# Gather, cumulative sum and projection: groups of 512 rows, a gather that converts to fp16 in flight, and stores in runs of 8 KB

## The chip, the cores and the metric

The kernel runs on one core of a Trainium2 chip. The metric is the device time of one execution in microseconds (us), as the median of several runs. Engines are named as in the profile: PE multiplies matrices, DVE and ACT are the vector and the scalar engine, POOL issues the gathers, SP issues plain transfers, and 16 DMA engines move the data.

## The reference

```
x: (16, 4096, 512) fp32    indices: (16, 2048) int64, sorted in each batch    w: (512, 512) fp32
gathered = x[b_idx, indices, :]          # (16, 2048, 512)
cs = np.cumsum(gathered, axis=1)         # along the 2048 rows
return np.matmul(cs, w)                  # (16, 2048, 512) fp32
```

67.1 MB of rows of 2 KB are gathered, and 67.1 MB of output are written.

## The kernel before

A batch of 2048 rows is 16 tiles of 128 rows. For each of the 16 batches the program makes three passes over its tiles.

- POOL gathers a tile's 128 rows of 2 KB into one slot of `g32` (L79), and ACT copies the slot to fp16, `g16` (L86). `g32` holds a whole batch and has two buffers, so the first gather of a batch waits until all casts of the batch two before it are done.
- PE multiplies each of four column blocks of `g16` with the upper triangular `ut` (L93, four matmuls of 128 columns). That gives the tile's cumulative sum, transposed, in the PSUM tile `pa`. DVE adds the last column of the tile before and writes fp16 `csT` (L106; L103 for the first tile, a plain copy). So the tiles of a batch form a chain on DVE.
- PE multiplies the four column blocks of `csT` with `w16` (L116, four matmuls of 512 columns, summed in `pb`). `pb` is copied to `ob` by DVE for even tiles (L125) and by ACT for odd ones (L127). SP stores `ob`, 128 rows of 2 KB (L128). There are 12 `ob` buffers.

The indices of a batch come as 16 rows of 128, are converted to fp32 (L62), transposed on PE (L64) and copied to unsigned integers (L66). Four batches are loaded before the loop and one more in each turn, on SP's queue behind the load of `w` (L51, cast on DVE at L52).

The framework puts each engine's instructions in order by priority, and each engine runs its own in that order. The adds have a raised priority (L101), so that they and the cumulative sums of a batch stand among the projections of the same batch; the last 22 projection matmuls of a batch stand behind all of its cumulative sums.

Of the kernel before, what the change touches and what calls it, by code (L numbers as in the profile page):

```python
# [1 line left out]

# [5 lines left out]

P = 128  # L10
FP32 = mybir.dt.float32
FP16 = mybir.dt.float16
U32 = mybir.dt.uint32


@with_exitstack
def kernel(
    ctx: ExitStack,
    tc: tile.TileContext,
    x: bass.AP,  # L20
    indices: bass.AP,
    w: bass.AP,
    out: bass.AP,
):
    nc = tc.nc

    B, S, D = x.shape
    N = indices.shape[1]
    assert D == 512 and N % P == 0

    NT = N // P
    DC = D // P
    PREF = 3

    x_flat = x.rearrange("b s d -> (b s) d")
    idx_u32 = indices.bitcast(U32)

    const = ctx.enter_context(tc.tile_pool(name="const", bufs=1))
    idxp = ctx.enter_context(tc.tile_pool(name="idxp", bufs=6))
    gp = ctx.enter_context(tc.tile_pool(name="gp", bufs=2))  # L40
    big = ctx.enter_context(tc.tile_pool(name="big", bufs=2))
    outp = ctx.enter_context(tc.tile_pool(name="outp", bufs=12))
    psA = ctx.enter_context(tc.tile_pool(name="psA", bufs=2, space=bass.MemoryType.PSUM))
    psB = ctx.enter_context(tc.tile_pool(name="psB", bufs=5, space=bass.MemoryType.PSUM))

    ut = const.tile([P, P], FP16)
    make_upper_triangular(nc, ut[:], 1.0, diag=True)

    w16 = const.tile([P, DC, D], FP16)
    w32 = const.tile([P, DC, D], FP32)  # L50
    nc.sync.dma_start(out=w32[:], in_=w.rearrange("(c p) d -> p c d", p=P))  # L51
    nc.vector.tensor_copy(out=w16[:], in_=w32[:])  # L52

    id16 = const.tile([16, 16], FP32)
    make_identity(nc, id16[:])
    idxgs = {}

    def load_indices(b):
        idx64 = idxp.tile([16, P], mybir.dt.int64, name="idx64")
        nc.sync.dma_start(out=idx64[:], in_=indices[b].rearrange("(t p) -> t p", p=P))  # L60
        idxf = idxp.tile([16, P], FP32, name="idxf")
        nc.vector.tensor_copy(out=idxf[:], in_=idx64[:].bitcast(U32)[:, 0::2])  # L62
        idx_ps = psB.tile([P, 16], FP32, name="idx_ps", tag="pb")
        nc.tensor.transpose(out=idx_ps[:], in_=idxf[:], identity=id16[:])  # L64
        idxg = idxp.tile([P, NT], U32, name="idxg")
        nc.vector.tensor_copy(out=idxg[:], in_=idx_ps[:])  # L66
        idxgs[b] = idxg

    for bb in range(4):
        load_indices(bb)  # L70

    for b in range(B):
        if b + 4 < B:
            load_indices(b + 4)
        idxg = idxgs.pop(b)
        g32 = gp.tile([P, NT, D], FP32, name="g32")
        g16 = big.tile([P, NT, D], FP16, name="g16")
        for t in range(NT):
            nc.gpsimd.indirect_dma_start(  # L79
                out=g32[:, t, :],  # L80
                out_offset=None,
                in_=x_flat,
                in_offset=bass.IndirectOffsetOnAxis(ap=idxg[:, t : t + 1], axis=0),
                element_offset=b * S * D,
            )
            nc.scalar.copy(out=g16[:, t, :], in_=g32[:, t, :])  # L86

        csT = big.tile([P, DC, N], FP16, name="csT")

        for t in range(NT):  # L90
            pa = psA.tile([P, DC * P], FP32, name="pa")
            for c in range(DC):
                nc.tensor.matmul(  # L93
                    out=pa[:, c * P : (c + 1) * P],
                    lhsT=g16[:, t, c * P : (c + 1) * P],
                    rhs=ut[:],
                    start=(c == 0),
                    stop=(c == DC - 1),
                )
            pa3 = pa[:].rearrange("p (c n) -> p c n", c=DC)  # L100
            with tc.high_priority(offset=200):  # L101
                if t == 0:
                    nc.vector.tensor_copy(out=csT[:, :, 0:P], in_=pa3)  # L103
                else:
                    carry = csT[:, :, t * P - 1 : t * P].broadcast_to([P, DC, P])
                    nc.vector.tensor_tensor(  # L106
                        out=csT[:, :, t * P : (t + 1) * P],
                        in0=pa3,
                        in1=carry,
                        op=mybir.AluOpType.add,  # L110
                    )

        for t in range(NT):
            pb = psB.tile([P, D], FP32, name="pb")
            for c in range(DC):
                nc.tensor.matmul(  # L116
                    out=pb[:],
                    lhsT=csT[:, c, t * P : (t + 1) * P],
                    rhs=w16[:, c, :],
                    start=(c == 0),  # L120
                    stop=(c == DC - 1),
                )
            ob = outp.tile([P, D], FP32, name="ob")
            if t % 2 == 0:
                nc.vector.tensor_copy(out=ob[:], in_=pb[:])  # L125
            else:
                nc.scalar.copy(out=ob[:], in_=pb[:])  # L127
            nc.sync.dma_start(out=out[b, t * P : (t + 1) * P, :], in_=ob[:])  # L128


# [1 line left out]
_INS = ['x', 'indices', 'w']  # L132
_OUTS = [((16, 2048, 512), 'float32')]


# [23 lines left out]
```

## Time and profile before

| | us |
|---|---|
| median of 3 runs (lowest, highest) | 381.35 (379.84, 381.68) |
| the profiled execution, its span | 595.4 |
| POOL busy issuing gathers | 242.8 |
| PE busy | 359.3 |
| DVE busy | 260.1 |
| ACT busy | 208.7 |
| mean granted clock of PE, as a share of full | 0.776 |

The profiled execution's own time is its span, 595.4 us; it is 1.56 times the median of the runs. Busy times are those of the profiled execution. Durations in the rows below are from it as well.

### The profile page before, as it was taken

To read this page: it belongs to the slowest core of one execution; us is meant where nothing else is said; L and a number is where in the kernel's file an instruction comes from. 1 tells how busy PE (TensorE), PEld (TensorE's weight loads), DVE (VectorE), ACT (ScalarE), POOL (GpSimd) and SP (SyncE) were. 2 spreads that over 40 slices of the span, in tenths; PEclk is the share of its full clock that TensorE was granted. 3 is DMA by queue.
4 is the path that set the end of the run, shared out by engine and by line. 5 is a ranking of instruction groups with operands and counts; after the bars stand their busy time and mean duration, and the time that the engine had idled before them with its cause. 6 is when DMAs were issued, how large, how long until landed. Compare 5 with 4: busy or idle time off the path is not lost.

```text
span 595.4 us, 6309 instructions
## 1 busy us (share of the span) xinstructions
PE 359.3 (60%) x2064; PEld 177.9 (30%) x2064; DVE 260.1 (44%) x417; ACT 208.7 (35%) x385; POOL 243.7 (41%) x264
## 2 busy tenths in 40 slices
PE   0413653746464791829558284582855838559997
PEld 0201231323232341414224142241422414225553
DVE  2202352425253572516327163361642717339885
ACT  1302353333160453307034070350703507045722
POOL 3772737372717254450714507236072360710000
PEclk9855967566969895868759677596785968869999
DMA  4774969584859678674857748568385684855565
GB/s 141 215 223 143 296 220 295 165 314 162 284 192 307 222 268 293 225 220 177 290 179 243 243 164 288 183 231 263 149 295 187 216 279 189 290 197 211 214 233 227
DMA packets 58416, 135.96 MB, mean 228 GB/s; under 512 B 8464, under 2 KB 8720, under 8 KB 58384
## 3 DMA queue, kind: packets, MB, share of 16 engines
q0 software_dynamic: 20480, 67.13, 37.2%
q1 hardware_dynamic: 37904, 68.44, 30.7%
q8 instruction: 16, 0.26, 0.2%
q14 instruction: 16, 0.13, 0.1%
HBM read 68.42 MB, written 67.11 MB: 228 GB/s over the span
## 4 chain that ended last, share of the span: by engine, by line
PE 49%; another core or an unknown queue 32%; issue 8%; DVE 7%; DMA 2%; POOL 1%; ACT 1%; DVEq 0%; ACTq 0%
PE pb L116 38%; PE pa L93 11%; DVE csT L106 3%; DVE csT L103 2%; DVE ob L125 2%; DMA w<-in_w_dram 1%; POOL g L79 1%; DMA g<-in_x_dram,idxg 1%; ACT ob L127 0%; ACT g L86 0%; DVE w L52 0%; PE idx_ps L64 0%; DVE idxf L62 0%; DVE idxg L66 0%
## 5 line engine op out<-in xcount | busy, mean ns | idle before, releaser
L79 POOL DMA_INDIRECT g<-in_x_dram,idxg x256 | 242.8, 949 | 280.0 <-ACT g L86 198.7
L116 PE MATMUL pb<-w,csT 128*128 128x512 f16 x1024 | 307.6, 434 | 18.9 <-DVE ob L125 13.1
L106 DVE TENSOR_TENSOR csT<-pa,csT 128x512 f16<-128x512 f32 x240 | 165.3, 689 | 148.9 <-remote 91.0
L93 PE MATMUL pa<-ut,g 128*128 128x128 f16 x1024 | 109.0, 238 | 196.1 <-DVE csT L106 91.9
L127 ACT COPY ob<-pb 128x512 f32<-128x512 f32 x128 | 75.1, 586 | 352.6 <-remote 163.8
L93 PEld LDWEIGHTS <-g 128*128 128x128 f16 x1024 | 81.7, 106 | 278.5 <-issue 188.1
L125 DVE COPY ob<-pb 128x512 f32<-128x512 f32 x128 | 87.7, 688 | 164.1 <-remote 87.9
L86 ACT CAST g<-g 128x512 f16<-128x512 f32 x256 | 141.8, 620 | 29.9 <-DMA g<-in_x_dram,idxg 16.5
L116 PEld LDWEIGHTS <-csT 128*128 128x128 f16 x1024 | 103.3, 110 | 111.6 <-issue 61.3
L64 PE MATMUL idx_ps<-id,idxf 16*128 16x16 f32 x16 | 3.4, 252 | 17.1 <-DVE idxf L62 8.3
L103 DVE CAST csT<-pa 128x512 f16<-128x512 f32 x16 | 11.0, 690 | 6.0 <-remote 2.6
L64 PEld LDWEIGHTS idx_ps<-id,idxf 16*128 16x128 f32 x16 | 2.3, 158 | 22.8 <-issue 11.4
L62 DVE CAST idxf<-idx 16x128 f32<-16x128 uint32 x16 | 3.2, 215 | 2.6 <-DMA idx<-in_indices_dram 2.4
L52 DVE CAST w<-w 128x2048 f16<-128x2048 f32 x1 | 1.2, 1227 | 6.8 <-DMA w<-in_w_dram 6.8
L66 DVE CAST idxg<-idx_ps 128x16 uint32<-128x16 f32 x16 | 2.5, 171 | 2.8 <-PE idx_ps L64 2.4
L86 ACT ACT_TABLE_LOAD x1 | 1.3, 1283 | 0.7 <-PEq L143 0.7
masks.py:65 POOL MEMSET ut<- 128x128 f16 x1 | 0.2, 205 | 0.3 <-POOLq L143 0.3
masks.py:66 POOL TENSOR_SCALAR_AFFINE_SELECT ut<-ut 128x128 f16<-128x128 f16 x1 | 0.3, 284 | 0.0
L143 POOL MEMSET const-float32-0.0<- 128x1 f32 x1 | 0.1, 104 | 0.2 <-issue 0.2
masks.py:199 POOL TENSOR_SCALAR_AFFINE_SELECT id<-id 16x16 f32<-16x16 f32 x1 | 0.2, 190 | 0.0
L143 POOL MEMSET const-uint8-127<- 128x1 uint8 x1 | 0.1, 124 | 0.0
L143 POOL MEMSET const-bfloat16-1.0<- 128x1 bf16 x1 | 0.1, 118 | 0.0
(2 smaller groups left out, 0.2 us busy)
## 6 DMA issues: line engine op xcount, KB each, us to landing
out_dram<-ob SPq DMA_DIRECT2D x256, 256.0 KB
g<-in_x_dram,idxg POOLq DMA_INDIRECT x256
w<-in_w_dram SPq DMA_DIRECT2D x1, 1024.0 KB
idx<-in_indices_dram SPq DMA_DIRECT2D x16, 16.0 KB
```

Of the source, the lines that this page charges most:

```text
L52: nc.vector.tensor_copy(out=w16[:], in_=w32[:])
L62: nc.vector.tensor_copy(out=idxf[:], in_=idx64[:].bitcast(U32)[:, 0::2])
L64: nc.tensor.transpose(out=idx_ps[:], in_=idxf[:], identity=id16[:])
L66: nc.vector.tensor_copy(out=idxg[:], in_=idx_ps[:])
L79: nc.gpsimd.indirect_dma_start(out=g32[:, t, :], out_offset=None, in_=x_flat, in_offset=bass.IndirectOffsetOnAxis(ap=idxg[:, t : t + 1], a ...
L86: nc.scalar.copy(out=g16[:, t, :], in_=g32[:, t, :])
L93: nc.tensor.matmul(out=pa[:, c * P : (c + 1) * P], lhsT=g16[:, t, c * P : (c + 1) * P], rhs=ut[:], start=(c == 0), stop=(c == DC - 1),)
L103: nc.vector.tensor_copy(out=csT[:, :, 0:P], in_=pa3)
L106: nc.vector.tensor_tensor(out=csT[:, :, t * P : (t + 1) * P], in0=pa3, in1=carry, op=mybir.AluOpType.add,)
L116: nc.tensor.matmul(out=pb[:], lhsT=csT[:, c, t * P : (t + 1) * P], rhs=w16[:, c, :], start=(c == 0), stop=(c == DC - 1),)
L125: nc.vector.tensor_copy(out=ob[:], in_=pb[:])
L127: nc.scalar.copy(out=ob[:], in_=pb[:])
```

## The change

These things are different, and the diff below holds them.

- The tiles of all batches form one sequence of 256, in 64 groups of four (512 rows). There are no passes by batch any more.
- The gather writes fp16 `g16` tiles directly from fp32 `x`; `g32` and ACT's casts are gone. There are 48 buffers of one tile. Ten groups (40 gathers) are issued before the loop, and one more group in each turn.
- The triangular `ut` has its columns permuted: column (r, q) sums the rows up to 4q + r of the tile. `csT` of a group is laid out so that the projection with index r uses the rows 4p + r of the group's 512 rows, for p from 0 to 127. Each partition of the output then holds four neighbouring rows.
- In the loop, the cumulative sum of tile r of group g stands ahead of projection r of group g - 1, in program order.
- `pa` has three buffers in place of two. DVE does all adds and no output copies.
- ACT does all output copies, into one `ob` tile of four rows per partition.
- A store takes the whole group, 1 MB with runs of 8 KB, from SP. There are five `ob` buffers.
- The indices come in two loads of 128 x 128, are converted, transposed and copied before the loop.
- `w` is loaded on ACT's queue and cast on ACT.

```diff
-    idxp = ctx.enter_context(tc.tile_pool(name="idxp", bufs=6))
-    gp = ctx.enter_context(tc.tile_pool(name="gp", bufs=2))
-    big = ctx.enter_context(tc.tile_pool(name="big", bufs=2))
-    outp = ctx.enter_context(tc.tile_pool(name="outp", bufs=12))
-    psA = ctx.enter_context(tc.tile_pool(name="psA", bufs=2, space=bass.MemoryType.PSUM))
+    gp = ctx.enter_context(tc.tile_pool(name="gp", bufs=R * (AHEAD + 2)))      # R = 4, AHEAD = 10
+    csp = ctx.enter_context(tc.tile_pool(name="csp", bufs=4))
+    outp = ctx.enter_context(tc.tile_pool(name="outp", bufs=5))
+    psA = ctx.enter_context(tc.tile_pool(name="psA", bufs=3, space=bass.MemoryType.PSUM))
...
+    for k in range(KI):                                                        # KI = 2
+        nc.sync.dma_start(out=idx64[:, k, :], in_=idx_rows[k * P : (k + 1) * P, :])
+    nc.scalar.dma_start(out=w32[:], in_=w.rearrange("(c p) d -> p c d", p=P))
+    make_identity(nc, ident[:])
+    nc.gpsimd.memset(ut[:], 1.0)                                               # ut: [P, R, Q], Q = 32
+    nc.gpsimd.affine_select(out=ut[:], in_=ut[:], compare_op=mybir.AluOpType.is_ge, fill=0.0,
+        base=0, pattern=[[1, R], [R, Q]], channel_multiplier=-1)
+    for k in range(KI):
+        nc.vector.tensor_copy(out=idxf[:, k, :], in_=idx64[:, k, :].bitcast(U32)[:, 0::2])
+        idx_ps = psB.tile([P, P], FP32, name="idx_ps", tag="pb")
+        nc.tensor.transpose(out=idx_ps[:], in_=idxf[:, k, :], identity=ident[:])
+        nc.vector.tensor_copy(out=idxg[:, k, :], in_=idx_ps[:])
-    nc.vector.tensor_copy(out=w16[:], in_=w32[:])
+    nc.scalar.copy(out=w16[:], in_=w32[:])
...
+    def gather(g):
+        for r in range(R):
+            t = g * R + r
+            g16 = gp.tile([P, D], FP16, name="g16")
             nc.gpsimd.indirect_dma_start(
-                out=g32[:, t, :],
+                out=g16[:],
...
-            nc.scalar.copy(out=g16[:, t, :], in_=g32[:, t, :])
...
+    def cumsum_tile(g, r):
+        pa = psA.tile([P, DC, R, Q], FP32, name="pa")
+        for c in range(DC):
+            nc.tensor.matmul(out=pa[:, c], lhsT=g16[:, c * P : (c + 1) * P], rhs=ut[:],
+                start=(c == 0), stop=(c == DC - 1))
+        dst = csT[:, :, :, r * Q : (r + 1) * Q]
...
+        nc.vector.tensor_tensor(out=dst, in0=pa[:],
+            in1=last.unsqueeze(2).broadcast_to([P, DC, R, Q]), op=mybir.AluOpType.add)
...
+    def project_tile(g, r):
+        for c in range(DC):
+            nc.tensor.matmul(out=pb[:], lhsT=csT[:, c, r, :], rhs=w16[:, c, :],
+                start=(c == 0), stop=(c == DC - 1))
+        nc.scalar.copy(out=obs[g][:, r, :], in_=pb[:])
+        if r == R - 1:
+            b, h = divmod(g, GB)                                               # GB = 4 groups in a batch
+            dst = out[b, h * R * P : (h + 1) * R * P, :].rearrange("(p j) d -> p j d", j=R)
+            nc.sync.dma_start(out=dst, in_=obs.pop(g)[:])
...
+    for g in range(AHEAD):
+        gather(g)
+    for g in range(G + 1):                                                     # G = 64
+        if g + AHEAD < G:
+            gather(g + AHEAD)
+        for r in range(R):
+            if g < G:
+                cumsum_tile(g, r)
+            if g > 0:
+                project_tile(g - 1, r)
```

## Rows read from the trace of the kernel before

**Rows 1.** The page: its first line, span and number of instructions.
```profile
span 595.4 us, 6309 instructions
```

**Rows 2.** Timeline of POOL, last 16 gathers: start us, us, instruction, idle time before.
```profile
504.58 0.94 POOL L79 DMA_INDIRECT g<-in_x_dram,idxg  x1 [15.26 <-ACT g L86]
505.83 0.94 POOL L79 DMA_INDIRECT g<-in_x_dram,idxg  x1 [0.30 <-issue]
...
523.38 0.95 POOL L79 DMA_INDIRECT g<-in_x_dram,idxg  x1 [0.30 <-issue]
```

**Rows 3.** Timeline of all engines, start.
```profile
0.75 0.44 SPq L51 DMA_DIRECT2D w<-in_w_dram  x1
...
7.90 0.75 DVE L62 CAST idxf<-idx 16x128 f32<-16x128 uint32 x5
...
9.03 1.10 POOL L79 DMA_INDIRECT g<-in_x_dram,idxg  x1 [7.55 <-DVE idxg L66]
...
12.63 0.62 ACT L86 CAST g<-g 128x512 f16<-128x512 f32 x1 [10.61 <-DMA g<-in_x_dram,idxg]
```

**Rows 4.** Waits of POOL: us in total, times, longest us.
```profile
POOL g L79 <- ACT g L86: 198.7, 14, 18.1
POOL g L79 <- issue: 73.1, 239, 0.6
```

**Rows 5.** Groups by line: busy us, mean ns of one, idle time before.
```profile
L79 POOL DMA_INDIRECT g<-in_x_dram,idxg x256 | 242.8, 949 | 280.0 <-ACT g L86 198.7 <-issue 73.1 <-DVE idxg L66 7.6
L106 DVE TENSOR_TENSOR csT<-pa,csT 128x512 f16<-128x512 f32 x240 | 165.3, 689 | 148.9 <-remote 91.0 <-PE pb L116 19.6 <-PE pa L93 18.2
L86 ACT CAST g<-g 128x512 f16<-128x512 f32 x256 | 141.8, 620 | 29.9 <-DMA g<-in_x_dram,idxg 16.5 <-PE pa L93 7.5 <-remote 3.7
...
L125 DVE COPY ob<-pb 128x512 f32<-128x512 f32 x128 | 87.7, 688 | 164.1 <-remote 87.9 <-PE pb L116 54.3 <-issue 20.9
L127 ACT COPY ob<-pb 128x512 f32<-128x512 f32 x128 | 75.1, 586 | 352.6 <-remote 163.8 <-PE pb L116 79.8 <-issue 63.7
L103 DVE CAST csT<-pa 128x512 f16<-128x512 f32 x16 | 11.0, 690 | 6.0 <-remote 2.6 <-PE pa L93 2.5 <-issue 0.9
```

**Rows 6.** Timeline of PE and DVE, a late start.
```profile
29.02 0.58 PE L93 MATMUL pa<-ut,g 128*128 128x128 f16 x4 [5.80 <-DVE ob L125]
...
39.51 0.69 DVE L106 TENSOR_TENSOR csT<-pa,csT 128x512 f16<-128x512 f32 x1 [10.64 <-remote]
```

**Rows 7.** Engines by stretch, two batches without gathers: last PEclk, DMA share, GB/s.
```profile
553.00:591.00 38.00, 36.88 (x261) 19.74 (x259) 31.84 (x49) 14.78 (x27) 0.00 (x0) 1.00 0.60 228
```

**Rows 8.** DMA queues, whole span: packets, MB, share of 16 engines' time.
```profile
q0 software_dynamic: 20480, 67.13, 37.2%
q1 hardware_dynamic: 37904, 68.44, 30.7%
```

**Rows 9.** DMA queues from 121.5 to 130 us.
```profile
DMA packets 1263, 3.20 MB, mean 376 GB/s; under 512 B 201, under 2 KB 201, under 8 KB 1263
...
q0 software_dynamic: 623, 2.04, 63.6%
q1 hardware_dynamic: 640, 1.15, 35.5%
```

**Rows 10.** DMA queues from 222 to 227 us.
```profile
q0 software_dynamic: 416, 1.37, 68.3%
q1 hardware_dynamic: 368, 0.66, 34.4%
```

**Rows 11.** DMA queues from 12 to 28 us, before the first store.
```profile
q0 software_dynamic: 1005, 3.31, 73.1%
```

**Rows 12.** Timeline of PE, the end.
```profile
587.70 3.62 PE L116 MATMUL pb<-w,csT 128*128 128x512 f16 x16
```

**Rows 13.** SP's stores: duration of an issue, min, median, max.
```profile
L128 SPq DMA_DIRECT2D out_dram<-ob x256: 332/332/1004, 28.3 to 592.0; - x128
```

**Rows 14.** DMA throughput from 0 to 10 us, in 40 equal slices.
```profile
GB/s 0 0 0 0 0 0 0 66 106 115 147 213 319 401 377 360 410 401 426 397 369 242 62 70 99 8 0 0 0 0 0 0 0 0 0 0 62 4 66 0
```

More of the change, by code (lines that the diff above doesn't have):

```diff
@@ L13 @@
 U32 = mybir.dt.uint32
+I64 = mybir.dt.int64
 @with_exitstack
@@ L28 @@
     N = indices.shape[1]
-    assert D == 512 and N % P == 0
+    R = 4
+    Q = P // R
+    DC = D // P
     NT = N // P
-    DC = D // P
-    PREF = 3
+    T = B * NT
+    G = T // R
+    GB = NT // R
+    AHEAD = 10
+    assert D == 512 and N % (R * P) == 0 and T % P == 0
     x_flat = x.rearrange("b s d -> (b s) d")
-    idx_u32 = indices.bitcast(U32)
     const = ctx.enter_context(tc.tile_pool(name="const", bufs=1))
-    idxp = ctx.enter_context(tc.tile_pool(name="idxp", bufs=6))
-    gp = ctx.enter_context(tc.tile_pool(name="gp", bufs=2))
@@ L41 @@
-    big = ctx.enter_context(tc.tile_pool(name="big", bufs=2))
-    outp = ctx.enter_context(tc.tile_pool(name="outp", bufs=12))
-    psA = ctx.enter_context(tc.tile_pool(name="psA", bufs=2, space=bass.MemoryType.PSUM))
-    psB = ctx.enter_context(tc.tile_pool(name="psB", bufs=5, space=bass.MemoryType.PSUM))
-    ut = const.tile([P, P], FP16)
-    make_upper_triangular(nc, ut[:], 1.0, diag=True)
-    w16 = const.tile([P, DC, D], FP16)
-    w32 = const.tile([P, DC, D], FP32)
-    nc.sync.dma_start(out=w32[:], in_=w.rearrange("(c p) d -> p c d", p=P))
@@ L52 @@
-    nc.vector.tensor_copy(out=w16[:], in_=w32[:])
[L54 to L78, printed above, removed]
+    gp = ctx.enter_context(tc.tile_pool(name="gp", bufs=R * (AHEAD + 2)))
+    csp = ctx.enter_context(tc.tile_pool(name="csp", bufs=4))
+    outp = ctx.enter_context(tc.tile_pool(name="outp", bufs=5))
+    psA = ctx.enter_context(tc.tile_pool(name="psA", bufs=3, space=bass.MemoryType.PSUM))
@@ new lines @@
+    psB = ctx.enter_context(tc.tile_pool(name="psB", bufs=5, space=bass.MemoryType.PSUM))
+    KI = T // P
+    idx_rows = indices.rearrange("b (t p) -> (b t) p", p=P)
+    idx64 = const.tile([P, KI, P], I64)
+    for k in range(KI):
+        nc.sync.dma_start(out=idx64[:, k, :], in_=idx_rows[k * P : (k + 1) * P, :])
+    w32 = const.tile([P, DC, D], FP32)
+    nc.scalar.dma_start(out=w32[:], in_=w.rearrange("(c p) d -> p c d", p=P))
+    ident = const.tile([P, P], FP32)
+    make_identity(nc, ident[:])
@@ new lines @@
+    ut = const.tile([P, R, Q], FP16)
+    nc.gpsimd.memset(ut[:], 1.0)
+    nc.gpsimd.affine_select(
+        out=ut[:],
+        in_=ut[:],
+        compare_op=mybir.AluOpType.is_ge,
+        fill=0.0,
+        base=0,
+        pattern=[[1, R], [R, Q]],
+        channel_multiplier=-1,
+    )
+    idxf = const.tile([P, KI, P], FP32)
+    idxg = const.tile([P, KI, P], U32)
+    for k in range(KI):
[3 more added lines that the diff above has]
+        nc.vector.tensor_copy(out=idxg[:, k, :], in_=idx_ps[:])
@@ L86 @@
-            nc.scalar.copy(out=g16[:, t, :], in_=g32[:, t, :])
[L88 to L128, printed above, removed]
+                in_offset=bass.IndirectOffsetOnAxis(ap=idxg[:, t // P, t % P : t % P + 1], axis=0),
@@ new lines, in gather @@
+                element_offset=(t // NT) * S * D,
+            )
+            gs[t] = g16
+    def cumsum_tile(g, r):
+        if r == 0:
+            cst[g] = csp.tile([P, DC, R, P], FP16, name="csT")
+        csT = cst[g]
+        g16 = gs.pop(g * R + r)
+        pa = psA.tile([P, DC, R, Q], FP32, name="pa")
+        for c in range(DC):
+            nc.tensor.matmul(
+                out=pa[:, c],
+                lhsT=g16[:, c * P : (c + 1) * P],
+                rhs=ut[:],
+                start=(c == 0),
+                stop=(c == DC - 1),
+            )
+        dst = csT[:, :, :, r * Q : (r + 1) * Q]
+        if g % GB == 0 and r == 0:
+            nc.vector.tensor_copy(out=dst, in_=pa[:])
+            return
+        if r == 0:
+            last = cst[g - 1][:, :, R - 1, P - 1 : P]
+        else:
+            last = csT[:, :, R - 1, r * Q - 1 : r * Q]
+        nc.vector.tensor_tensor(
+            out=dst,
+            in0=pa[:],
+            in1=last.unsqueeze(2).broadcast_to([P, DC, R, Q]),
+            op=mybir.AluOpType.add,
+        )
@@ new lines @@
+    obs = {}
+    def project_tile(g, r):
+        if r == 0:
+            obs[g] = outp.tile([P, R, D], FP32, name="ob")
+        csT = cst[g]
+        pb = psB.tile([P, D], FP32, name="pb")
+        for c in range(DC):
+            nc.tensor.matmul(
+                out=pb[:],
+                lhsT=csT[:, c, r, :],
+                rhs=w16[:, c, :],
+                start=(c == 0),
+                stop=(c == DC - 1),
+            )
+        nc.scalar.copy(out=obs[g][:, r, :], in_=pb[:])
[3 more added lines that the diff above has]
+            nc.sync.dma_start(out=dst, in_=obs.pop(g)[:])
```

7 lines of the change are left out of this document (4 added, 3 removed).

## The prediction

> **What bounds the kernel now.** I read in this order: the span against the median, the waits of the engine that issues the gathers, the busy time of the engines, and the DMA queues, whole and by stretch.
>
> The profiled execution spans 595.4 us [rows 1]; that is its own time, and the median of the runs is 381.35 us. So first the reader must separate what the profile's waits cost from what its work costs. POOL issues 256 gathers, one each 1.25 us (0.95 busy and 0.30 to the next) [rows 2], from 9.03 us [rows 3] to 524.3 us. In that stretch it waits 198.7 us for the casts on ACT and 73.1 us for nothing that the profile shows [rows 4]. Start 9.0, busy 242.8 [rows 5], issue 73.1 and that wait make 523.6; the rest to 595.4 is a tail of 71 us. Of the median 9.0 + 315.9 are POOL's as well, which leaves 56 us for the wait and the tail that take 270 us in the profile. So the waits here are mostly the profiled execution's own, and I don't count them. What they are shows in one place: the four short matmuls at 29.02 are over by 29.6, and the DVE add that reads their sums starts at 39.51, after 10.6 us put down to "remote" [rows 6]. Durations of work I do use.
>
> By work, ACT is at 141.8 + 75.1 = 217 us, DVE at 165.3 + 87.7 + 11 = 264 [rows 5]. PE at its full clock of 2.4 GHz (granted 1.00, in a stretch where no gather runs) does 261 recorded matmuls, two batches, in 38 us with 36.9 busy [rows 7]: 19 us a batch, 304 us in all. POOL needs 321. All four are well under 381. The DMA engines aren't. 67.13 MB go through the gathers' queue and 68.44 through the other [rows 8]: 135.6 MB, and over 381.35 us that is 356 GB/s. In the profile the only stretches near that are those where both queues are full: 376 GB/s over 8.5 us with 63.6 + 35.5 = 99% of the 16 engines' time [rows 9], and 68.3 + 34.4% over a fuller 5 us [rows 10]. From the second I take prices. A gather's 4096 bytes take 0.683 x 5 us x 16 / (1.37 MB / 4096) = 163 ns of an engine; 2048 bytes of a store take 0.344 x 80 us / (0.66 MB / 2048) = 85 ns. The first stretch gives 174 and 86 the same way.
>
> One tile of 128 rows is 256 KB in and 256 KB out, 16 KB of each per engine: 4 x 163 + 8 x 85 = 1.33 us by the fuller stretch, 1.38 by the longer. 256 tiles are 341 or 354 us. With 9.0 until the first gather, 3.6 until its data are used (9.03 to 12.63, [rows 3]), about 3 for a ramp in which gathers run alone at 73% share [rows 11], and a tail of about 10 (cast 0.62, cumsum 0.58, add 0.69, the 22 projections that stand last on PE at 3.62 / 16 = 0.226 [rows 12], copy 0.69, store and landing 2), the kernel should take 367 to 380. I read the median as DMA engines that are full, or nearly, with up to 14 us lost to waits between batches.
>
> **The change part by part.** *Casts leave ACT.* ACT loses 141.8 us, takes over DVE's 128 copies at 586 ns (75 us more): 150 us plus one copy of w. DVE loses 87.7. Neither set the end, so these are worth nothing by themselves; they are covered by the DMA engines' 341 us. What they free is POOL: it no longer waits for ACT. It waits for tiles that PE has read, with 48 buffers, 40 of them issued ahead; nothing else is queued behind it on POOL but gathers.
>
> *The gather converts in flight.* No row shows such a transfer. It reads the same 2 KB rows and writes 1 KB. Bounds: if an engine's time goes with the bytes written, 82 ns for the 4096 read; if each element must pass twice, 327. I take 163, the plain row: the read side is unchanged and is the larger. POOL's issue is also unseen for this form; the nearest row is 0.95 + 0.30, below it nothing suggests a gain since the 128 rows stay 128, above it twice the busy part. I take the row: 321 us.
>
> *Stores in 8 KB runs.* Four tiles make one store, 1 MB, 64 instead of 256. SP's issue of 332 ns [rows 13] is hidden either way. Per 8 KB the bounds are 4 x 85 = 340 ns, and 307 ns from the best quarter microsecond of the load of w, 426 GB/s [rows 14] (8192 / (426 / 16) = 308). I take 320: 20 ns less, two per tile and engine, 256 tiles: 10 us saved.
>
> *Order on PE.* Four short and four long matmuls alternate per tile, in the same numbers as before; 256 tiles at 19/16 us are 304 us, under the DMA engines. The cumsum of tile t stands in front of a projection, so a late gather now stops projections too; they are of the group before, and what waits for them are stores. At 1.3 us a tile PE is 90% busy, so I leave the clock at its upper level. The permuted columns give the DVE add runs of 32 instead of 128; I keep 689 ns, 176 us in all. Twice that would be 353 us and DVE would be the bound.
>
> *Start.* Two index loads of 128 KB replace sixteen of 16 KB, of which the first stood behind w's 1 MB; w moves to ACT's queue, so on SP nothing is ahead of the indices. Before, the first index cast starts at 7.90 behind w and the gather at 9.03, 1.1 us later [rows 3]. The first bytes of w flow at 1.75 us, 1.0 after its issue [rows 14]; 128 KB beside w cannot be done before about 3, nor later than w did. I take the first gather at 6.0 (bounds 4.5 and 9.0). The two transposes, the mask and the identity lie in that time. The conversion of w on ACT has until the first projection, some 15 us.
>
> *End.* After the last gather's data: cumsum 0.6, add 0.69, 16 projections 3.6 [rows 12], copy 0.59, issue 0.33, 1 MB at the stores' price 2.6, and 2 for the way there and back (an estimate: w's way there is 1.0): 10.4, of which the 2.6 are in the DMA sum.
>
> **The sum.** DMA: 256 x (4 x 0.163 + 2 x 0.320) = 331 us. 6.0 + 3.6 + 331 + 3 + 7.8 = 351. The same sum for the kernel before came to 367 with these prices, 14 short of the median. What those 14 are I can't read: if full engines are simply dearer over long stretches, the new kernel pays them too (365); if they were POOL's waits for casts and the 12 store buffers, it pays none (351). I take half: **358 us**.
>
> **The memory's share as a rival rule.** In the fuller 8.5 us the queues moved 376 GB/s [rows 9] and w's load reached 426 [rows 14], so the average of 356 is not a ceiling by these rows. If it were one, the same 135 MB would take the same time, 380 us: the bytes of memory do not change, only those written on chip. The Trainium skill, page "SBUF — State Buffer", section "Summary: rules for kernel authors", says to estimate transfers between HBM and SBUF with about 358 GB/s; by that the time would be 135.6 MB / 358 = 379 us, before and after. The rows above go over it, so I give it little weight.
>
> **Rivals.**
> 1. *The DMA engines stay full, gathers at about the plain price* (forecast): 358, from 345 to 370. Chance 0.50.
> 2. *POOL becomes the bound*, because half the bytes written makes a gather cheaper than 0.150 us per 4096: 6.0 + 256 x 1.25 + 3.6 + 10.4 = 340, from 335 to 345. For it: 1.25 against 1.29 us a tile is already close. Against: reads are the larger side. Chance 0.22.
> 3. *The conversion is dear on the DMA engines.* Each ns per 4096 bytes is 4 x 256 = 1.02 us, so 23 ns more than 163 (186 ns, 14%) takes back everything, and at the upper bound of 327 the time is 358 + 168 = 526 us. For it: no row shows the form, and the engines are full, so nothing hides it. Against: nothing in the rows says that it costs at all. Chance 0.17, slower than before.
> 4. *Average of 356 GB/s is a ceiling*: 380, same. Chance 0.06.
> 5. Between 370 and 379 (dearer packets, a wait of PE on late gathers): 0.05.
>
> A difference under 0.5% (1.9 us) can't be told from no change here. Faster: 0.50 + 0.22 + 0.05 = 0.77; same 0.06; slower 0.17. The range takes 1, 2, 5 and 4, from 336 to 383; what is left out is mostly rival 3.
>
> **What the new profile would show.** The step on ACT: no wait of POOL for ACT, ACT near 150 us, DVE near 177. The gather's price: in a stretch where both queues together hold over 95% of the engines' time, the time of the gathers' queue per byte read, 163 ns for 4096 read; 186 or more and the forecast is wrong on the far side, 140 and POOL sets the end. POOL: 1.25 us from gather to gather; if its busy part grows, the floor of 340 goes up by 0.256 us per ns. Stores: 8 KB packets at 308 to 340 ns. Start: first gather at 4.5 to 9 us. The span of the new profile may again stand far over its median; then the prices count, not the span.

## The result, and the profile after

| | us |
|---|---|
| changed kernel, median of 6 runs (lowest, highest) | 359.89 (357.66, 366.29) |
| kernel before, beside it, median of 6 runs | 381.51 (379.84, 383.58) |
| ratio, 95% interval | 0.942 (0.937 to 0.947) |
| predicted | 358, range 336 to 383 |

The change made the kernel 5.8% faster, as forecast. Ratios, here and below, leave out executions more than 1.5% above the fastest of the same kernel, and the profiled one is such a one (366.29 us, the longest of its six; its span is 364.5). In two of the four groups of experiments the kernel before took 562 to 573 us where it takes 381 in the others, for a reason that stays open; each run below stands beside the kernel before of its own group.

The page of the changed kernel answers to [rows 1, 5, 8]: span, DMA queues (packets, MB, share of 16 engines' time), groups by line, and DMA issues (median us from issue to landing).

```profile
span 364.5 us, 5566 instructions
...
q0 software_dynamic: 36864, 33.57, 59.5%
q1 hardware_dynamic: 9504, 67.38, 45.7%
...
L90 POOL DMA_INDIRECT g<-in_x_dram,idxg x256 | 240.3, 939 | 104.5 <-issue 39.0
...
L121 DVE TENSOR_TENSOR csT<-pa,csT 128x512 f16<-128x512 f32 x240 | 166.0, 692 | 156.5 <-PE pa L106 156.1
L143 ACT COPY ob<-pb 128x512 f32<-128x512 f32 x256 | 150.1, 586 | 201.1 <-PE pb L136 200.3
L106 PE MATMUL pa<-ut,g 128*128 128x128 f16 x1024 | 102.3, 224 | 53.6 <-DMA g<-in_x_dram,idxg 53.1
...
out_dram<-ob SPq DMA_DIRECT2D x64, 1024.0 KB, 7.3
g<-in_x_dram,idxg POOLq DMA_INDIRECT x256, 8.2
```

Three things are to be seen. The gathers' queue counts 33.57 MB, the bytes it writes, and it has 36864 packets where the plain gathers have 20480 [rows 8]. In either number 4096 are small ones (16 a gather); the 32768 rows of 2 KB then make 16384 plain packets of two rows, or 32768 converted ones of one row. The two shares sum to 105% over the whole span, so times of packets overlap. And PE waits 53 us for gathers to land: data, not an engine, is late.

The waits of POOL for gathers (us in total, times, longest), which answer to [rows 4], have no line for ACT. POOL now waits for the landing of earlier gathers, or for PE's reading of a tile.

```profile
POOL g L90 <- issue: 39.0, 128, 0.3
POOL g L90 <- PE pa L106: 26.3, 49, 3.2
POOL g L90 <- DMA g<-in_x_dram,idxg: 23.6, 48, 1.9
POOL g L90 <- PE pb L136: 9.9, 30, 1.1
POOL g L90 <- DVE idxg L78: 5.5, 1, 5.5
```

A stretch in the middle, 100 to 140 us, read like [rows 9, 10]: packets, MB, share.

```profile
DMA packets 5487, 11.95 MB, mean 299 GB/s; under 512 B 604, under 2 KB 4520, under 8 KB 4520
...
q0 software_dynamic: 4406, 4.01, 63.3%
q1 hardware_dynamic: 1079, 7.91, 48.6%
```

4.01 MB written in packets of 1024 B are 3916 rows. 0.633 x 40 us x 16 / 3916 = 103 ns for a row, or 207 per 4096 bytes read, where I took 163. A store's 8192 bytes take 0.486 x 640 us / (7.91 MB / 8192) = 322 ns, where I took 320. But the shares sum to 112%. Counted by what the kernel asks of memory, 8.02 MB read and 7.91 written, the stretch moves 398 GB/s.

### The profile page after: what moved, and what is told of

It reads as the page before. It is cut to its first block, busy times and chain, and to the rows that moved or that the text cites. A ratio compares the mean times of both kernels' runs of the same rounds, so it can differ in the third digit from the quotient of the medians.

```text
span 364.5 us, 5566 instructions
## 1 busy us (share of the span) xinstructions
PE 298.8 (82%) x2050; PEld 155.0 (43%) x2050; DVE 178.1 (49%) x260; ACT 153.2 (42%) x258; POOL 241.4 (66%) x264
## 3 DMA queue, kind: packets, MB, share of 16 engines
q0 software_dynamic: 36864, 33.57, 59.5%
## 4 chain that ended last, share of the span: by engine, by line
DMA 50%; PE 30%; POOL 12%; issue 6%; POOLq 0%; ACT 0%; DVE 0%; SPq 0%
DMA g<-in_x_dram,idxg 48%; PE pb L136 23%; POOL g L90 12%; PE pa L106 7%; DMA idx<-in_indices_dram 1%; POOLq L185 0%; ACT ob L143 0%; SPq L53 0%; DVE idxf L75 0%; DVE idxg L78 0%; POOLq L90 0%
## 5 line engine op out<-in xcount | busy, mean ns | idle before, releaser
L90 POOL DMA_INDIRECT g<-in_x_dram,idxg x256 | 240.3, 939 | 104.5 <-issue 39.0
L136 PE MATMUL pb<-w,csT 128*128 128x512 f16 x1024 | 267.2, 385 | 0.0
L143 ACT COPY ob<-pb 128x512 f32<-128x512 f32 x256 | 150.1, 586 | 201.1 <-PE pb L136 200.3
L106 PE MATMUL pa<-ut,g 128*128 128x128 f16 x1024 | 102.3, 224 | 53.6 <-DMA g<-in_x_dram,idxg 53.1
L106 PEld LDWEIGHTS <-g 128*128 128x128 f16 x1024 | 74.2, 99 | 132.5 <-DMA g<-in_x_dram,idxg 90.5
L136 PEld LDWEIGHTS <-csT 128*128 128x128 f16 x1024 | 91.0, 99 | 64.2 <-issue 4.3
L77 PE MATMUL idx_ps<-ident,idxf 128*128 128x128 f32 x2 | 0.9, 461 | 6.4 <-DVE idxf L75 6.4
L81 ACT CAST w<-w 128x2048 f16<-128x2048 f32 x1 | 1.9, 1899 | 3.8 <-DMA w<-in_w_dram 3.8
```

The source lines that it names most:

```text
L77: nc.tensor.transpose(out=idx_ps[:], in_=idxf[:, k, :], identity=ident[:])
L81: nc.scalar.copy(out=w16[:], in_=w32[:])
L90: nc.gpsimd.indirect_dma_start(out=g16[:], out_offset=None, in_=x_flat, in_offset=bass.IndirectOffsetOnAxis(ap=idxg[:, t // P, t % P : t % ...
L106: nc.tensor.matmul(out=pa[:, c], lhsT=g16[:, c * P : (c + 1) * P], rhs=ut[:], start=(c == 0), stop=(c == DC - 1),)
L136: nc.tensor.matmul(out=pb[:], lhsT=csT[:, c, r, :], rhs=w16[:, c, :], start=(c == 0), stop=(c == DC - 1),)
L143: nc.scalar.copy(out=obs[g][:, r, :], in_=pb[:])
```

## The experiments

**Theories.** *A*: an edit moves the time by the price of its packets on the DMA engines. *B*: the bytes moved set the time, so neither the conversion nor the 8 KB runs do anything. *C*: the gain is that of the order, one sequence of tiles in place of passes by batch. A fourth, *D*, came after the first runs: the edits add up. (E, F, G and L in the expectations came later still; each says there what it is.) Two edits of the changed kernel can be undone apart, the converting gather and the 8 KB stores; with both undone, what is left is order, buffers and start. Undoing the converting gather also puts the casts back on ACT, so its price below is that of both together.

**Plain gather, 8 KB stores** (e1, f1). ACT casts three tiles ahead of their use, and DVE takes half of the output copies back.

```diff
-            g16 = gp.tile([P, D], FP16, name="g16")        # target of the gather
+            g32 = gp.tile([P, D], FP32, name="g32")
...
+            nc.scalar.copy(out=g16[:], in_=gs.pop(t)[:])   # for tile t + 3, g16 from a pool of 8
...
-        nc.scalar.copy(out=obs[g][:, r, :], in_=pb[:])
+        if r % 2 == 0:
+            nc.vector.tensor_copy(out=obs[g][:, r, :], in_=pb[:])
+        else:
+            nc.scalar.copy(out=obs[g][:, r, :], in_=pb[:])
```

> The changed kernel with one part undone: the gather moves fp32 (2 KB rows on both sides), ACT casts each tile (256 more operations), and DVE takes half of the output copies. Theory A, the DMA engines are full and a converted row costs them 98 ns instead of about 80: the gathers' queue falls from 217 us of engine time to about 167, the sum of both queues from 383 to 334, and the time to POOL's own pace, 7 + 319 + 18, so 344 to 350 us. Theory B, the memory's bytes set the pace (135 MB at about 375 GB/s): the bytes are the same, so 358 to 362. Theory C, the order of work on PE and the pace of POOL set it and the DMA engines don't: 358 to 362 too, with gathers that land in less time.

> fp32 gathers cast on ACT, all else as in the changed kernel; it took 472 us where the kernel before takes 562. Where the kernel before takes 381: theory A (full DMA engines, a converted row costs 98 ns against 80) 344 to 350 us; theory B (bytes of memory) and theory C (order on PE and POOL's pace) 358 to 362 us. Theory L, where the kernel before takes 562: 465 to 475 again, because more signals between engines are needed for each tile.

**Converting gather, 2 KB stores** (e2, f2). A store a tile, in runs of 2 KB, 256 of them. The runs of one store lie 8 KB apart in memory, where the kernel before stores 256 KB in one piece.

```diff
-    outp = ctx.enter_context(tc.tile_pool(name="outp", bufs=5))
+    outp = ctx.enter_context(tc.tile_pool(name="outp", bufs=20))     # tiles of [P, D]
...
-            nc.sync.dma_start(out=dst, in_=obs.pop(g)[:])
+        nc.sync.dma_start(out=dst[:, r, :], in_=ob[:])
```

> The changed kernel with one part undone: each tile is stored by itself, 256 KB in runs of 2 KB, 256 stores, 20 buffers of one tile. Theory A: 8 x 85 ns per tile and engine in place of 2 x 321, 38 ns more, 256 tiles: 10 us more, 368 to 372 us. Theory B: same bytes, 358 to 362. Theory C: 358 to 362.

> Stores of 256 KB in runs of 2 KB, all else as in the changed kernel; it took 447 us where the kernel before takes 562. Where the kernel before takes 381: theory A 368 to 372 us (10 us more engine time), B and C 358 to 362. Theory L on the other kind of chip: 447 again and equal to the control.

**Both undone** (e3, h3): the two edits above together. **One store in four** (e4, f4): the changed kernel with three quarters of the output not stored.

```diff
-        if r == R - 1:
+        if r == R - 1 and g % 4 == 3:
```

> The changed kernel with both parts undone: fp32 gathers cast on ACT, and stores of 2 KB runs. What is left of the change is one sequence of tiles with deep buffers, the earlier start, and the order on PE. Theory A: gathers 163 ns per 4096 bytes and stores 85 per 2048, 343 us of engine time, POOL's pace of 344 nearly hidden in it: 352 to 362. Theory B: 358 to 362. Theory C: 358 to 362. If the time comes near that of the kernel before, 378 to 384, then the order and the buffers gave nothing and the 8 KB stores gave all.

> fp32 gathers cast on ACT and stores of 2 KB runs: of the change only the one sequence of tiles, its buffers, the start and the order on PE are left. On a chip where the kernel before takes 381 us, the 8 KB stores were worth 14.6 us beside converted gathers (375.4 against 360.8) and the conversion nothing (360.5). Theory D, these add up and the order gives the rest: 374 to 377 us. Theory A, only the engines' time counts and plain gathers are cheaper: 360 to 366. Theory E, the order and the buffers give nothing: 380 to 383, and then the conversion gave the last 5 us beside stores of 2 KB.

> The changed kernel with three of four stores left out (48 of 64 groups are computed and copied but not stored). Theory A: the engines' time is 217 + 42 us, far under the span, so POOL's pace is left: 7 + 319 + 18 = 344 us, with gathers that land in about 3.5 us and no wait of POOL between gathers. Theory B: 85 MB, same 344. Theory C: 356 to 362, nothing changes, because PE still runs the same order and POOL the same gathers.

> Three of four stores left out, all else as in the changed kernel. Where the kernel before takes 381: theory A, POOL's pace is left, 7 + 319 + 18 = 344 us, gathers land in about 3.5 us; B the same 344; C 356 to 362. Theory L on the other kind of chip: 445 again, equal to the control though the bytes stored are a quarter.

**Controls**: the changed kernel again, and the kernel before with a profile.

> The changed kernel itself, as the control beside the others. The first four experiments ran on a chip on which the kernel before takes 562 us, not 381. If this chip is like that one, theory L (signals between engines arrive late while POOL issues gathers, and that sets the time there) expects 440 to 450 us, the same as with stores of 2 KB (447) or a quarter of the stores (445). If it is like the one of the result, 358 to 362 us.

> The kernel before itself, for a profile on a chip where it takes 381 us; the rows ahead of the prediction span 595. Prediction's reading: both queues together above 95% of the engines' time in the steady part, adds on DVE that start at once after PE's sums and no wait put down to remote of more than 3 us, POOL's wait for ACT under 40 us in place of 199. Theory C: engines' time under 90% and POOL's wait for ACT the larger part of 56 us. On a chip where it takes 562: the same picture as in the rows, 200 us of POOL waiting for ACT.

Measured, beside a kernel before of 381 us (f0, f1, f2 and f4 on one chip; h0 and h3 in another group), and beside one of 562 us:

| | us | ratio (95%) | beside 562 | ratio |
|---|---|---|---|---|
| both undone (h3, e3) | 362.72 | 0.951 (0.947 to 0.955) | 477.47 | 0.852 |
| plain gather, 8 KB stores (f1, e1) | 360.47 | 0.949 (0.943 to 0.955) | 472.38 | 0.841 |
| converting gather, 2 KB stores (f2, e2) | 375.42 | 0.984 (0.979 to 0.989) | 447.26 | 0.798 |
| the changed kernel (f0) | 360.83 | 0.944 (0.937 to 0.951) | | |
| one store in four (f4, e4) | 343.65 | 0.901 (0.896 to 0.906) | 444.87 | 0.793 |
| kernel before, one run, profiled (h0) | 380.77 | | | |

Beside 381 us each theory fails on a row. A wanted a plain gather to be cheaper than the changed kernel (344 to 350 with 8 KB stores); it isn't. B and C wanted the 2 KB stores to cost nothing beside a converting gather; they cost 14.6 us (375.4 - 360.8; 15.2 by the ratios, 0.040 x 381). C also wanted 356 to 362 with a quarter of the stores; it is 343.65. D wanted 374 to 377 with both edits undone; it is 362.7. B comes nearest: apart from the 2 KB stores beside a converting gather, it is never out by more than 1 us. The edits interact. Order, buffers and start alone bring 18.2 us (380.9 to 362.7). The conversion then costs 12.7 us (375.4 - 362.7) and the 8 KB runs, beside it, give 14.6 back. Beside plain gathers they are worth 2.2, which the intervals don't tell from nothing.

The four kernels stand in the order of their DMA packets: 24.6, 41.0, 49.2 and 65.5 thousand rows' and stores' packets (16384 or 32768 for the gathers, 8192 or 32768 for the stores) at 360.5, 360.8, 362.7 and 375.4 us. But the kernel before has as many as the third of them (49.2) and takes 381, and no run varied the count by itself. Why the conversion and the 2 KB runs cost so much only together stays open.

The Trainium skill, page "Perfetto Trace Analysis", section "DMA Optimizations", says that batching transfers from 2 KB into 4 or 8 KB can raise the throughput a great deal. Here 8 KB runs bring 14.6 of 375 us (3.9%) beside gathers of one row a packet, and 2.2 us beside gathers of two.

**Where the order's gain comes from.** The kernel before, now at 380.77 us: waits of POOL, its last gather, then its engines by stretch (us, length, PE busy and matmuls, PEld, DVE, ACT, POOL, granted clock, DMA share, GB/s).

```profile
POOL g L79 <- issue: 72.8, 239, 0.3
...
POOL g L79 <- ACT g L86: 2.1, 7, 0.3
```

```profile
327.44 0.95 POOL L79 DMA_INDIRECT g<-in_x_dram,idxg  x1 [0.30 <-issue]
```

```profile
30.00:120.00 90.00, 64.81 (x397) 32.67 (x397) 49.98 (x80) 52.59 (x93) 68.02 (x72) 0.91 1.00 352
120.00:328.00 208.00, 187.59 (x1276) 98.85 (x1275) 155.98 (x247) 129.51 (x239) 157.43 (x167) 0.98 1.04 406
328.00:379.00 51.00, 45.57 (x312) 23.89 (x311) 38.53 (x59) 20.18 (x37) 0.39 (x1) 1.00 0.71 269
```

POOL issues back to back, 1.249 us a gather from 8.66 to 328.4; the 198.7 us of [rows 4] are 2.1. So the casts held no gather up, and the gathers came at POOL's pace, not at that of the DMA engines. But 51 us are left after the last gather, with the DMA engines at 71%: PE still has 312 recorded matmuls to do, over two batches. The same stretches with both edits undone:

```profile
30.00:120.00 90.00, 79.77 (x550) 43.33 (x551) 67.66 (x103) 58.34 (x105) 68.07 (x73) 0.98 1.03 387
120.00:328.00 208.00, 177.25 (x1249) 96.61 (x1249) 153.05 (x234) 134.09 (x240) 157.27 (x167) 1.00 1.04 402
```

```profile
326.92 0.94 POOL L91 DMA_INDIRECT g<-in_x_dram,idxg  x1 [0.30 <-ACT g L105]
```

The gathers end at 327.9, 0.5 us before those of h0, but PE did 550 matmuls from 30 to 120 us where the kernel before did 397, and 33.7 us are left in place of 50.6. Those 16.9 us are nearly all of the 18.2. The backlog arises in that early stretch. Waits from 30 to 120 us, two of the kernel before, then one with both edits undone:

```profile
ACT g L86 <- DMA g<-in_x_dram,idxg: 33.5, 41, 3.7
...
PE pb L116 <- ACT ob L127: 22.0, 11, 3.9
```

```profile
PE pb L144 <- ACT ob L154: 6.8, 8, 1.6
```

PE is idle for 25.2 of these 90 us in the kernel before, and 22.0 of them it waits for ACT's output copies. The kernel before at 65 us:

```profile
65.12 0.62 ACT L86 CAST g<-g 128x512 f16<-128x512 f32 x1 [3.66 <-DMA g<-in_x_dram,idxg]
65.64 0.58 ACT L127 COPY ob<-pb 128x512 f32<-128x512 f32 x1
...
66.27 1.01 PE L116 MATMUL pb<-w,csT 128*128 128x512 f16 x2 [3.90 <-ACT ob L127]
```

ACT stands 3.66 us in front of a cast whose gather hasn't landed; the output copy behind it is late, and PE, which needs the `pb` buffer that the copy frees, waits 3.90 us. The eleven waits above are all of this kind: each time the copy stands on ACT behind a cast that has waited for its gather, 0.38 to 3.66 us. Buffers are not what is short there: from 30 to 120 us no copy waits for a store and POOL waits for no cast longer than 0.3 us. Later copies do wait for stores, 68.1 us in all (38.9 on ACT, 29.2 on DVE) with 12 output buffers, but 67.2 us (34.6 and 32.6) with the 20 of h3. So the traces point to the order of casts and copies on ACT; no run beside 381 us put the casts elsewhere in the kernel before, so the order is not shown apart from the rest.

**Where the conversion's cost is.** Queues of the plain gather with 8 KB stores (f1), from 120 to 240 us; then of the converting gather with 2 KB stores (f2), and of the kernel before (h0), in the same stretch.

```profile
DMA packets 10835, 48.93 MB, mean 408 GB/s; under 512 B 1873, under 2 KB 1873, under 8 KB 7865
...
q0 software_dynamic: 7493, 24.55, 53.0%
q1 hardware_dynamic: 3329, 24.23, 48.1%
```

```profile
DMA packets 25210, 34.57 MB, mean 288 GB/s; under 512 B 2802, under 2 KB 13985, under 8 KB 25199
...
q0 software_dynamic: 12583, 11.46, 57.6%
q1 hardware_dynamic: 12616, 22.97, 55.8%
```

```profile
DMA packets 20686, 48.98 MB, mean 408 GB/s; under 512 B 2976, under 2 KB 2976, under 8 KB 20675
...
q0 software_dynamic: 7680, 25.18, 52.2%
q1 hardware_dynamic: 12995, 23.67, 51.4%
```

Doubling the converting queue's MB for the bytes it reads, f2 moves (2 x 11.46 + 22.97) MB / 120 us = 382 GB/s, 6% under the 408 of both plain ones; 135.6 MB at 382 take 355 us, at 408 332. The kernel before runs at 408 with 2 KB stores as f1 does with 8 KB ones, so longer runs by themselves don't raise the rate. Nor does f1, at 408 here, end ahead of the changed kernel: from 30 to 120 us it moves 382 GB/s, and 410 only after that. The share doesn't tell these stretches apart as the rate does: the kernel before stands at a share of 1.00 from 30 to 120 us, where it moves 352 GB/s, and at 1.04 from 120 to 328, where it moves 406. So a share near 1 is no sign by itself that the engines can move no more.

With a quarter of the stores (f4), POOL sets the end. Its queues over the whole span and its last gather:

```profile
q0 software_dynamic: 36864, 33.57, 73.4%
q1 hardware_dynamic: 2592, 17.04, 13.1%
```

```profile
325.33 0.94 POOL L90 DMA_INDIRECT g<-in_x_dram,idxg  x1 [0.30 <-PE pa L106]
```

Gathers go from 8.10 to 326.3 us, 1.243 each, and 16.2 us are left: 343.65 where rival 2 had 340. The changed kernel's 361 less 344 is what three quarters of its stores cost; without them the two shares sum to 86.5% in place of 105%.

**The other 200 us.** Two more kernels were meant for the condition in which the kernel before takes 381 us, and ran in the other: the kernel before with 20 output buffers in place of 12, and the plain gather with the cast one tile ahead, each half of the indices converted by itself, and the last group stored by tiles.

> The kernel before with 20 output buffers in place of 12, as many tiles as in the changed kernel. With fp32 gathers and 2 KB stores the new order and buffers alone took 362.7 us against 380.9. Theory F, the 12 buffers held the work back (ACT and DVE wait 68 us for stores): 364 to 372 us. Theory G, ACT's casts of the next batch stand ahead of output copies and stop PE early on, so that two and a half batches are left when the last gather is issued at 328 us, and PE's pace of 19 us a batch sets the rest: 378 to 382 us, with 45 us or more from the last gather to the end.

> A version meant to beat both: fp32 gathers cast on ACT, each cast one tile ahead of its sum and behind the copy of the turn, 8 KB stores except the last group (one store a tile), and the first half of the indices converted before the second is waited for. Plain gathers with 8 KB stores took 360.5 us with casts three tiles ahead. Theory G: fewer copies stand behind a late gather, PE keeps up from the start, first gather at about 5 us in place of 8, last gather issued at about 332, 13 us more to the end: 343 to 349 us. If the DMA engines are full at a given sum of bytes whatever the order: 355 to 360.

The first took 572.49 us, ratio 0.988 (0.979 to 0.998), the second 471.29, ratio 0.837 (0.830 to 0.844), beside 572.91. Neither tells what these edits do where the kernel before takes 381. g1 was meant to beat the changed kernel, and that stays untested. One expectation can be read there anyway: g1's first gather, expected at about 5 us.

```profile
7.31 1.10 POOL L95 DMA_INDIRECT g<-in_x_dram,idxg  x1 [5.57 <-DVE idxg L81]
```

It starts at 7.31 us, no earlier than the changed kernel's 7.29.

The condition doesn't belong to a chip: these two ran on the chip (0) on which h0 and h3 had run, where the kernel before took 380.89. The profile of the kernel before with 20 buffers has the waits of [rows 4, 6] again:

```profile
ACT ob L127 <- remote: 189.4, 19, 15.4
POOL g L79 <- ACT g L86: 178.1, 14, 17.3
...
DVE csT L106 <- remote: 87.5, 21, 18.2
```

What happens there shows best in one kernel in both conditions, a quarter of the stores, 50 to 75 us: first beside 562 us (e4), with DVE's only line in that stretch, then beside 381 (f4).

```profile
50.00:75.00 25.00, 0.58 (x4) 0.32 (x3) 0.69 (x1) 0.58 (x1) 18.90 (x21) 0.50 0.83 106
```

```profile
67.48 0.69 DVE L121 TENSOR_TENSOR csT<-pa,csT 128x512 f16<-128x512 f32 x1 [22.42 <-issue]
```

```profile
50.00:75.00 25.00, 23.04 (x171) 12.80 (x170) 14.53 (x22) 12.29 (x21) 18.90 (x21) 1.00 0.92 150
```

POOL issues 21 gathers both times. PE, DVE and ACT do almost nothing in the one and run on in the other; DVE stands 22 us at a point where the profile shows nothing that it waits for. PE's granted clock is 0.50 of full there, its lower level of 1.2 GHz, after PE had stood idle. In that condition the conversion saves 30 us (477.5 to 447.3). The stores count for little: 447 with all in 2 KB runs and 445 with a quarter, and 5 us for 8 KB runs beside plain gathers (477.5 to 472.4). What holds the engines up there was not found.

## Why the prediction was right

The time was right (358 for 359.9), in part by luck: the mechanism, full DMA engines, held for the changed kernel, but the gather's price, the worth of the stores and the 14 us of waits were mis-sized, and their errors cancelled.

- *DMA engines full*: right for the changed kernel. PE waits 53 us for gathers, the rate stays near 390 to 400 GB/s, and with fewer stores the time falls to POOL's floor. For the kernel before it was right from 120 to 328 us: from 120 to 240 the prices are again 163 ns (0.522 x 120 us x 16 / (25.18 MB / 4096)) and 85 (0.514 x 1920 us / (23.67 MB / 2048)). It was wrong for the last 51 us, with the share at 0.71, and from 30 to 120, with the rate at 352. Of the 56 us that the prediction left for POOL's wait and the tail together, 50.6 are tail.
- *Casts leave ACT, no wait of POOL for ACT*: right (ACT 153.2 us busy, DVE 178.1, predicted 150 and 177). "What they free is POOL" was wrong: POOL waited 2.1 us for casts in h0.
- *The gather's price, taken at the plain row's 163 ns*: **mis-sized**. It is 207 in the changed kernel and 198 in f2 (0.576 x 1920 us for 11.46 MB, 99 ns a row), past the 186 from which I called the kernel not faster. The threshold was wrong too: it took packet times as if they lay end to end, and with converted gathers they overlap to 112%. By time, the conversion costs 12.7 us beside 2 KB stores, and beside 8 KB ones nothing that the runs can tell (360.8 against 360.5).
- *Stores*: the price was right, 322 ns for 320. Their worth, 10 us by the sum, is 14.6 beside converted gathers and 2.2 beside plain ones.
- *The 14 us, half of them recovered*: mis-sized and of another kind. By the traces they were neither dear engines nor POOL's waits, but a backlog of output that the passes by batch build up. Order, buffers, start and end brought 18.2, where I had 12 (7 for the waits, 3 for the start, 2 for the end). So the sum came out because errors cancelled: a gain 6 us too small for the order and 4.6 too small for the stores, against a cost of 12.7 left out for the conversion; together 2 us.
- *"The waits here are mostly the profiled execution's own"*: leaving them out of the sum was right, the reason wrong. The long waits come back in runs whose median, without a profile, is 562 to 573 us. They belong to a condition of the runs, not to profiling.
- *POOL*: right, 0.94 + 0.30 us, also for a gather that converts; and f4 comes within 4 us of its floor (343.65 for 340).
- *Start*: within bounds (7.29 for 6.0). The 3 us booked for it came to little: h3's gathers start at 7.89, 0.8 us before those of h0, and end 0.5 us before them. DVE converts the second half of the indices, which lands later, ahead of the copy that the first gather needs:

```profile
3.60 0.23 DVE L75 CAST idxf<-idx 128x128 f32<-128x128 uint32 x1 [3.60 <-DMA idx<-in_indices_dram]
...
6.58 0.23 DVE L75 CAST idxf<-idx 128x128 f32<-128x128 uint32 x1 [2.75 <-DMA idx<-in_indices_dram]
6.72 0.28 DVE L78 CAST idxg<-idx_ps 128x128 uint32<-128x128 f32 x1
...
7.29 1.09 POOL L90 DMA_INDIRECT g<-in_x_dram,idxg  x1 [5.55 <-DVE idxg L78]
```

- *End*: right. In the changed kernel the last gathered tile is read by PE at 354.03, and the span ends 10.5 us later, for 10.4.

```profile
354.03 0.40 PE L106 MATMUL pa<-ut,g 128*128 128x128 f16 x4
```

- *Rival 4, 356 GB/s as a ceiling*: refuted, 408 GB/s for 120 us in the kernel before. By the Trainium skill's 358 GB/s (page "SBUF — State Buffer", section "Summary: rules for kernel authors") the 48.98 MB of that stretch would take 137 us (an estimate); they took 120. The Trainium skill's page "HBM Reference", section "Specifications (TRN2)", says that a core which streams alone goes well above that share, to about 425; with that the traces agree.

No kernel that stores all of the output was clearly faster than the changed one: f1 can't be told from it, within either interval.

## What to carry to other kernels

Undo the parts of a change one by one and also together: here the largest part of the gain came from order, buffers and start together, and two of the edits cancelled. A kernel whose DMA share is full on average may still end on a backlog; look at the stretch after the last load and ask which early wait built it up. Prices per packet are good for finding a bound, not as a sum, once the shares of the queues go over 100%. And read the rate beside the share: a share near 1 came with 352 GB/s and with 406 here.

## What the runs showed of the hardware

- A gather that converts fp32 to fp16 moves one row of 2 KB in a packet, 103 ns each beside 8 KB stores and 99 beside 2 KB ones, where a plain one moves two in 163 ns. With 2 KB stores beside it, memory traffic is 382 GB/s for 408.
- Packet times of two full queues sum to as much as 113% of the 16 engines' time (57.6 + 55.8, f2).
- POOL issues an indirect gather of 128 rows each 1.243 to 1.249 us, converting or not (f4, h0).
- The same kernel, f4 and e4, takes 343.65 or 444.87 us; in e4 DVE stands 22 us with nothing shown that it waits for, while POOL goes on issuing gathers. One chip had the kernel before at 381 us and later at 573.
